# Rows of h at one place for the retention and at another for everything after it

## The chip, the cores and the metric

The kernel runs on one core of one Trainium2 chip. A core has a matrix engine (TensorE, PE in the profile; its loads of the stationary operand are shown as PEld), a vector engine (VectorE, DVE), a scalar engine (ScalarE, ACT), a general one (GpSimd, POOL) and a sync engine (SyncE, SP) that here issues the transfers. They run side by side and wait for each other by semaphores. The metric is device time in microseconds of one execution.

## The reference, cut to what matters

A trunk of two decoder layers over 256 tokens of width 2048, in float32. Layer 0 mixes tokens by retention, layer 1 by a short gated convolution; each mixer is followed by a SwiGLU feed-forward part.

```python
for i in range(DEPTH):                     # DEPTH = 2
    mod = (c_act @ w_mod[i] + b_mod[i])[:, None, :]
    sh1, sc1, g1, sh2, sc2, g2 = jnp.split(mod, 6, axis=-1)
    h = (rms_norm(x, norm1_g[i]) * (1.0 + sc1) + sh1)
    y = retention_mixer(...) if i == 0 else short_conv_mixer(...)
    x = x + g1 * y
    h = (rms_norm(x, norm2_g[i]) * (1.0 + sc2) + sh2)
    x = x + g2 * swiglu(h, ffn_w_in[i], ffn_w_out[i])
return rms_norm(x, final_g)
```

Retention has 8 heads with keys of 256 and values of 512; one projection gives q, k, v and a gate, with 12,288 columns in all. `h` is the input of each projection: 16 rows of 128 features by 256 tokens.

## The kernel before

**Precision.** Every float32 operand is split in two parts of a reduced float32 type: `hi`, the rounded value, and `lo`, what is left. A product takes hi by hi, hi by lo and lo by hi. For weights ACT makes `hi` (L313) and DVE makes `lo` (L316), in pieces of 128 x 1024, from `raw` tiles of 1 MB that SP fetches in the order of use. An activation row is one tile of 128 x 2 x 256: its hi half, then its lo half.

**Three forms of the product.** In `product` (L358, L361) the weights are loaded into the array and a whole row, 512 columns, streams past `hi`, then its hi half, 256 columns, past `lo`. It serves the output projections and the later stages. In `packed` (L398 to L400) the weights are loaded too, and the three partial products are three matmuls of 256 columns. In `by_token` (L373 to L375, called by `packed` for groups 512 columns wide: the retention's values and gates) it is the other way round: 128 tokens of h are loaded, and 512 columns of weights stream past them. Each of these lines has 512 matmuls with h in the retention.

**Stages.** The retention's input comes first, in spans of columns while h is still being made (to about 190 us), then head by head. Half of its output product stands in the middle and half at the end (to 786 us). Then come the feed-forward part of layer 0 (to 1521 us), the convolution (to 1880 us), the feed-forward part of layer 1, and the final norm.

**The rows of h.** One tile, `h_all`, holds 16 rows. `h[j]` is the view of 512 elements that starts at 512 j. A second view of the same tile, `raw_all`, has a stride of 514 elements: 2 (`ENDS`) for a shift column in hi and lo, and then a scaled row. It is used at the start of a normed projection, before the norm of x is known. While the output product before it ends, `scaled_only` writes row j of `raw_all` as soon as x[j] is ready (ACT L495 the hi half, DVE L496 the lo half). `normed` then copies the shift columns to all 16 rows at once (ACT L507, DVE L508) and multiplies the first group of columns with the scaled rows (L521 to L523). The norm's factor comes in between, and `modulated` writes the finished rows `h[j]` over the scaled ones, a few behind the matmuls that read those. This happens three times: for the feed-forward part of layer 0, for the convolution, and for the feed-forward part of layer 1. L521 and L523 stream the two shift columns as well, 258 columns, and L522 streams 256.

**What sets the order.** PE's instructions stand as the program writes them. DVE and ACT have an order by hand in the retention's start alone; elsewhere a scheduler places an instruction by priority and by what it depends on, that is by which regions of which tiles it reads and writes. The reductions for the modulation (L247, each over a 1 MB `raw` tile) are among those it fills in. Each engine runs its instructions in the built order and stops at one whose semaphores have not come. PE does not pass a matmul that waits.

**Places in the memory.** A tile `aside` of `LEFT` elements stands ahead of `h_all`, and a tile `beside` fills up behind it, so that the tiles which come later keep their places.

Of the kernel before, what the change touches and what calls it, by code (L numbers as in the profile page):

```python
# [10 lines left out]
F32 = mybir.dt.float32  # L11
F32R = mybir.dt.float32r
# [5 lines left out]
P = 128  # L18
D = 2048
S = 256  # L20
KT = D // P
# [27 lines left out]
STEPS = (8, 8, 20)  # L49
RAW_BUFS = 3  # L50
PART_BUFS = 4
LEFT, ENDS = 8, 2

Q0, K0, V0, G0 = 0, HEADS * DK, 2 * HEADS * DK, 2 * HEADS * DK + HEADS * DV
SH1, SC1, GT1, SH2, SC2, GT2 = range(6)
# [133 lines left out]
def trunk(ctx: ExitStack, tc: tile.TileContext, x_in, c_in, pos_in, w_mod, cols_in, tab_in, w_all, out):  # L189
# [12 lines left out]
    def tmp(tag, shape=(P, S), dtype=F32, pool=work, bufs=None):  # L202
        return pool.tile(list(shape), dtype, tag=tag, name=name(tag), bufs=bufs)
# [276 lines left out]
    hpool = ctx.enter_context(tc.tile_pool(name="hpool", bufs=1))  # L480

    hpool.tile([P, LEFT], F32, tag="aside", name="aside")
    h_all = hpool.tile([P, KT * (ENDS + 2 * S)], F32R, tag="h", name="h")
    hpool.tile([P, P - KT * ENDS], F32, tag="beside", name="beside")
    h = [h_all[:, 2 * S * j : 2 * S * (j + 1)].rearrange("p (a b) -> p a b", a=2) for j in range(KT)]
    raw_all = h_all.rearrange("p (k n) -> p k n", k=KT)

    def scaled_only(layer, norm, j):  # L490

        needed(layer, SC2 if norm else SC1, j)
        a = mod_a[layer][norm][:, j : j + 1]
        high, low = raw_all[:, j, ENDS : ENDS + S], raw_all[:, j, ENDS + S :]
        nc.scalar.activation(high, x[j], AF.Identity, scale=a)  # L495
        nc.vector.scalar_tensor_tensor(low, x[j], a, high.bitcast(F32), op0=ALU.mult, op1=ALU.subtract)  # L496
# [50 lines left out]
    def output(groups, act, which, last, after=None, base=None):  # L547

        layer, gate = which[0], mod_g[which[0]][which[1] == GT2]
        first, *groups = groups  # L550
        base, acc = first.ks[0] if base is None else base, None
        banks = product(first, act, base, last=False)
        for j, g in enumerate(groups):
            needed(*which, j)
            col = gate[:, j : j + 1]
            if last and j == KT - 1:
                (pt,) = packed(g, act, base)
                nc.vector.scalar_tensor_tensor(x[j], pt[:, 0, :], col, x[j], op0=ALU.mult, op1=ALU.add)
                acc = [acc, squares(None, x[j], "acc1")]
                if after:  # L560
                    after(j)
                return acc
            (pt,) = product(g, act, base, banks=banks[j : j + 1])
            t = tmp("sum", bufs=4)
            nc.vector.scalar_tensor_tensor(t, pt[:, 1, :], col, x[j], op0=ALU.mult, op1=ALU.add)
            nc.vector.scalar_tensor_tensor(x[j], pt[:, 0, :], col, t, op0=ALU.mult, op1=ALU.add)
            if last:
                acc = squares(acc, x[j])
            if after:
                after(j)  # L570


    with ExitStack() as inner:
# [357 lines left out]
        def ret_out(part, last):  # L931
            after = (lambda j: scaled_only(0, 1, j)) if last else None
            acc = output(RET_OUT[part], mid, (0, GT1), last, after, base=0)
            assert not asides
            for n in range(len(mid)):
                if ("mid", n) in tag_of:
                    free.append(tag_of.pop(("mid", n)))
            return acc

        for n, head in enumerate(HEAD_ORDER):  # L940
            projections(head)
            if n == HEADS // 2 - 1:
                ret_out(0, False)
        acc = ret_out(1, True)

    mpool = ctx.enter_context(tc.tile_pool(name="mpool", bufs=1))

# [30 lines left out]
    for i, g in enumerate(CONV_IN):  # L978
        pending += [sums(g)] if i else normed(acc, 1, 0, g)
        while len(pending) >= 3:  # L980
            pb, pc, pu = pending[:3]
            pending = pending[3:]
            j = done
            b, c, u = pb(tmp("bsum", pool=mpool, bufs=2)), pc(), pu()
# [73 lines left out]
```

## Time and profile before

| what | us |
|---|---|
| runs, median of 3 | 2629.78 (2628.91 to 2632.28) |
| the profiled execution | 2630.33 |
| its span, first to last instruction | 2628.6 |

The profile is of one execution. Its span is what the trace covers; the execution's own time lies 1.7 us above it. In a row of a group the figures after the bar are busy time, mean duration of one instruction in ns, and the idle time of the engine just before such instructions, with what ended it. A row of the timeline has start, duration, engine, line, operation and tiles; `x3` means that three were merged. A row of a window has the window, its length, the busy time and count of PE, of PEld, of DVE, of ACT and of POOL (only those of PE where the view was cut to that engine), and then the granted TensorE clock as a share of full speed, the busy share of the DMA engines, and GB/s. A matmul's duration is longer than its share of the stream, because neighbours overlap; what one costs is the pitch from its start to the start of the next.

### The profile page before, as it was taken

Reading aid. Unit: us, or ns where it says so; the run is one execution under the profiler, and the core shown is the slowest. Engines: PE = TensorE matmul, PEld = TensorE weight load, DVE = VectorE, ACT = ScalarE, POOL = GpSimd, SP = SyncE. Lnnn points to the kernel's source line nnn. Section 1 sums busy time; section 2 is a strip of 40 time slices with the busy share of each in tenths; the row PEclk is TensorE's granted clock in tenths of the full one; section 3 lists DMA queues with packets and bytes.
Section 4 is the critical chain, followed back from the end, with each engine's and each line's share of the span. In section 5 each row is a group of like instructions: output and inputs, shape, how many; then the busy total and the mean of one; then the engine's idle time right before and its main releaser. Section 6 shows DMA issues by size and latency. Waiting matters only on the chain.

```text
span 2628.6 us, 38238 instructions
## 1 busy us (share of the span) xinstructions
PE 2596.0 (99%) x15220; PEld 2301.1 (88%) x15220; DVE 1988.8 (76%) x2527; ACT 1249.2 (48%) x1788; POOL 149.8 (6%) x230
## 2 busy tenths in 40 slices
PE   7999999999999999999999999999999999999998
PEld 5888889888899888888888898888998888888887
DVE  7898878777698877777777889888887665555554
ACT  5544443444456444344444454444554443444443
POOL 0000001110000001101100001100000000000000
PEclk9999999999999999999999999999999999999999
DMA  9976668767686877777777758777777665555553
GB/s 398 386 279 239 249 246 305 284 258 274 240 297 247 322 287 275 285 284 282 284 271 278 282 214 330 288 272 268 260 268 267 252 223 192 193 191 187 187 190 127
DMA packets 96950, 687.58 MB, mean 262 GB/s; under 512 B 10753, under 2 KB 12545, under 8 KB 13825
## 3 DMA queue, kind: packets, MB, share of 16 engines
q1 hardware_dynamic: 96770, 685.13, 70.3%
q8 instruction: 119, 1.95, 0.3%
q14 instruction: 61, 0.50, 0.1%
HBM read 682.99 MB, written 2.10 MB: 261 GB/s over the span
## 4 chain that ended last, share of the span: by engine, by line
PE 76%; issue 20%; DVE 2%; DMA 1%; ACT 1%; POOL 0%; DVEq 0%; ACTq 0%; POOLq 0%
PE bank L358 34%; PE bank L361 18%; PE bank L373 4%; PE bank L374 4%; PE bank L375 4%; PE bank L400 2%; PE bank L398 2%; PE bank L399 2%; PE bank L521 1%; PE bank L523 1%; PE bank L522 1%; DVE raw L649 1%; DMA raw<-w_all 1%; DVE lo L316 1%; PE bank L876 1%
## 5 line engine op out<-in xcount | busy, mean ns | idle before, releaser
L316 DVE TENSOR_TENSOR lo<-raw,hi 128x1024 fp32r<-128x1024 f32 x912 | 1111.8, 1222 | 537.5 <-ACT hi L313 533.3
L313 ACT CAST hi<-raw 128x1024 fp32r<-128x1024 f32 x912 | 953.5, 1050 | 1066.7 <-PE bank L358 641.5
L358 PE MATMUL bank<-h,hi 128*128 128x512 f32 x3296 | 1142.8, 390 | 0.0
L361 PE MATMUL bank<-h,lo 128*128 128x256 f32 x3296 | 929.5, 282 | 0.0
L358 PEld LDWEIGHTS bank<-h,hi 128*128 128x128 f32 x3296 | 618.4, 188 | 129.5
L361 PEld LDWEIGHTS bank<-h,lo 128*128 128x128 f32 x3296 | 622.9, 189 | 0.0
L358 PE MATMUL bank<-mid,hi 128*128 128x512 f32 x1604 | 556.3, 390 | 0.0
L361 PE MATMUL bank<-mid,lo 128*128 128x256 f32 x1604 | 452.4, 282 | 0.9 <-DVE lo L316 0.9
L247 DVE SCALAR_TENSOR_TENSOR raw<-raw,cb 128x2048 f32<-128x2048 f32 x160 | 365.4, 2284 | 15.9 <-DMA raw<-w_mod 15.7
L358 PEld LDWEIGHTS bank<-mid,hi 128*128 128x128 f32 x1604 | 300.9, 188 | 63.1
L361 PEld LDWEIGHTS bank<-mid,lo 128*128 128x128 f32 x1604 | 303.1, 189 | 1.2 <-DVE lo L316 1.2
L373 PE MATMUL bank<-hi,h 128*128 128x512 f32 x512 | 204.4, 399 | 0.0
L374 PE MATMUL bank<-lo,h 128*128 128x512 f32 x512 | 203.8, 398 | 0.0
L375 PE MATMUL bank<-hi,h 128*128 128x512 f32 x512 | 203.6, 398 | 0.0
L358 PE MATMUL bank<-rm,hi 128*128 128x512 f32 x496 | 172.5, 390 | 0.0
L400 PE MATMUL bank<-h,lo 128*128 128x256 f32 x512 | 144.6, 282 | 8.3 <-DVE lo L316 8.3
L398 PE MATMUL bank<-h,hi 128*128 128x256 f32 x512 | 145.0, 283 | 2.5 <-ACT h L677 2.5
L399 PE MATMUL bank<-h,hi 128*128 128x256 f32 x512 | 144.4, 282 | 0.5 <-DVE h L678 0.5
L361 PE MATMUL bank<-rm,lo 128*128 128x256 f32 x496 | 139.8, 282 | 0.0
L375 PEld LDWEIGHTS bank<-hi,h 128*128 128x128 f32 x512 | 97.0, 189 | 23.5
L373 PEld LDWEIGHTS bank<-hi,h 128*128 128x128 f32 x512 | 97.0, 189 | 20.2
L374 PEld LDWEIGHTS bank<-lo,h 128*128 128x128 f32 x512 | 97.0, 189 | 20.1
(154 smaller groups left out, 2243.7 us busy)
## 6 DMA issues: line engine op xcount, KB each, us to landing
raw<-w_all SPq DMA_DIRECT2D x456, 1024.0 KB, 4.9
raw<-w_mod SPq DMA_DIRECT2D x192, 1024.0 KB, 5.0
x<-x_in SPq DMA_DIRECT2D x4, 512.0 KB, 5.8
out<-out SPq DMA_DIRECT2D x5, 256.0 KB, 3.4
decay<-tab_in SPq DMA_DIRECT2D x8, 128.0 KB, 2.8
out<-out SPq DMA_DIRECT2D x3, 128.0 KB, 2.5
out<-out SPq DMA_DIRECT2D x1, 384.0 KB, 2.7
cols<-cols_in SPq DMA_DIRECT2D x1, 160.0 KB, 9.0
```

The costliest lines, as they stand in the source:

```text
L247: nc.vector.scalar_tensor_tensor(raw, raw, 1.0, cb, op0=ALU.mult, op1=ALU.mult, accum_out=total)
L313: nc.scalar.copy(hi, raw)
L316: nc.vector.tensor_tensor(lo, raw, hi.bitcast(F32), op=ALU.subtract)
L358: nc.tensor.matmul(pt, hi, h, start=fresh and k == g.ks[0], stop=False, skip_group_check=True)
L361: nc.tensor.matmul(pt[:, 1, :], lo, h[:, 0, :], start=False, stop=last and k == g.ks[-1], skip_group_check=True)
L373: nc.tensor.matmul(o, ht[:, 0, :], hi, start=first, stop=False)
L374: nc.tensor.matmul(o, ht[:, 0, :], lo, start=False, stop=False)
L375: nc.tensor.matmul(o, ht[:, 1, :], hi, start=False, stop=last)
L398: nc.tensor.matmul(pt, hi, h[:, 0, :], start=first, stop=False, skip_group_check=True)
L399: nc.tensor.matmul(pt, hi, h[:, 1, :], start=False, stop=False, skip_group_check=True)
L400: nc.tensor.matmul(pt, lo, h[:, 0, :], start=False, stop=last, skip_group_check=True)
L521: nc.tensor.matmul(pt, hi, high, start=k == 0, stop=False, skip_group_check=True)
```

## The change

`h_all` grows by 16 elements (`LATER`), and its place is chosen so that element 16 lies where element 0 lay, seen in a grid of 512 bytes. `raw_all` starts at element 16. The rows `h[j]` start at element 0, 64 bytes lower, while the retention's projections run, and at element 16 from the end of the retention's output product on. Tiles allocated later move up by 512 bytes. No instruction is added or taken away.

```diff
-LEFT, ENDS = 8, 2
+LEFT, ENDS, LATER = 120, 2, 16
...
     hpool.tile([P, LEFT], F32, tag="aside", name="aside")
-    h_all = hpool.tile([P, KT * (ENDS + 2 * S)], F32R, tag="h", name="h")
-    hpool.tile([P, P - KT * ENDS], F32, tag="beside", name="beside")
-    h = [h_all[:, 2 * S * j : 2 * S * (j + 1)].rearrange("p (a b) -> p a b", a=2) for j in range(KT)]
-    raw_all = h_all.rearrange("p (k n) -> p k n", k=KT)
+    h_all = hpool.tile([P, LATER + KT * (ENDS + 2 * S)], F32R, tag="h", name="h")
+    hpool.tile([P, 2 * P - LEFT - LATER - KT * ENDS + 8], F32, tag="beside", name="beside")
+
+    def rows_at(o):
+        return [
+            h_all[:, o + 2 * S * j : o + 2 * S * (j + 1)].rearrange("p (a b) -> p a b", a=2) for j in range(KT)
+        ]
+
+    h = rows_at(0)
+    raw_all = h_all[:, LATER:].rearrange("p (k n) -> p k n", k=KT)
...
         acc = ret_out(1, True)
+        h = rows_at(LATER)
```

`h` is read at the time of each call, so `normed`, `modulated` and `sums` use the new list from there on.

## The prediction, on record before the changed kernel ran

> **What bounds the kernel now.** I read the page first, then the rate of TensorE (PE) in single stages, then the three places at which the built order of instructions differs.
>
> ```profile
> span 2628.6 us, 38238 instructions
> ...
> PE 2596.0 (99%) x15220; PEld 2301.1 (88%) x15220; DVE 1988.8 (76%) x2527; ACT 1249.2 (48%) x1788; POOL 149.8 (6%) x230
> ...
> L358 PE MATMUL bank<-h,hi 128*128 128x512 f32 x3296 | 1142.8, 390 | 0.0
> L361 PE MATMUL bank<-h,lo 128*128 128x256 f32 x3296 | 929.5, 282 | 0.0
> ...
> L358 PE MATMUL bank<-mid,hi 128*128 128x512 f32 x1604 | 556.3, 390 | 0.0
> ...
> L373 PE MATMUL bank<-hi,h 128*128 128x512 f32 x512 | 204.4, 399 | 0.0
> ...
> L358 PE MATMUL bank<-rm,hi 128*128 128x512 f32 x496 | 172.5, 390 | 0.0
> ...
> L398 PE MATMUL bank<-h,hi 128*128 128x256 f32 x512 | 145.0, 283 | 2.5 <-ACT h L677 2.5
> ```
>
> PE is busy through 99% of the span, with hardly any idle time before its lines. So the end is set by two things alone: the pitch from one matmul's start to the next, and each stop of PE. The last column of the L373 row is zero idle. The change touches both: the pitch, because rows of h that PE reads lie elsewhere, and the stops, because instructions change places.
>
> The pitch is read from starts in the timeline, since the mean duration holds latency. In order: packed rows (L398 to L400), value and gate columns by token (L373 to L375), and the product of the later stages (L358, L361).
>
> ```profile
> 455.72 0.28 PE L398 MATMUL bank<-h,hi 128*128 128x256 f32 x1
> ...
> 456.42 0.28 PE L398 MATMUL bank<-h,hi 128*128 128x256 f32 x1
> ...
> 457.46 0.40 PE L373 MATMUL bank<-hi,h 128*128 128x512 f32 x1
> ...
> 458.86 0.40 PE L373 MATMUL bank<-hi,h 128*128 128x512 f32 x1
> ```
> ```profile
> 859.91 0.39 PE L358 MATMUL bank<-h,hi 128*128 128x512 f32 x1
> 860.14 0.28 PE L361 MATMUL bank<-h,lo 128*128 128x256 f32 x1
> ...
> 861.30 0.39 PE L358 MATMUL bank<-h,hi 128*128 128x512 f32 x1
> ```
>
> Six packed matmuls take 0.70 us, 116.7 ns each; six by token take 1.40 us, 233.3 ns each. In the product the 512-wide one takes 0.23 us and four pairs take 1.39 us, so the same width costs about 5 ns less than by token.
>
> **The change, part by part: the place of h.** In the built program the split weights hi and lo start 352 bytes past a multiple of 512. The rows of h start at 384, and in the retention at 320 afterwards. The rows that later stages read keep 384, as do mid and the retention's own tiles, which move up by just 512 bytes. That move is free as far as the trace can tell: rows of h, and the tiles of mid and rm, sit on different multiples of 512, and all their L358 have one length, 390 ns in the three rows above. So only the retention's 3 x 512 packed and 3 x 512 by-token matmuls can change pitch, 1536 of each.
>
> No row of before has h at 320, so both terms are bounded.
>
> - By token, h is the loaded operand and the weights stream. Lower end: the attention's product L876, also 512 wide.
>
> ```profile
> 224.80 1.30 PE L876 MATMUL bank<-v,sp 128*128 128x512 f32 x5
> ```
>
> Five of these span 1.30 us; less one duration of 0.39 us, that is 0.91 us over four pitches, 227.5 ns: -5.8 ns a matmul, -8.9 us in all. Upper end: the product's saving with its sign turned, +5 ns, +7.7 us.
> - In the packed rows h streams. Lower end: half of the L876 pitch for half the columns, 113.8 ns, -2.9 ns, -4.5 us. For rows at other places there is the normed product (L521 to L523), whose 16 rows each lie 8 bytes further in the 64-byte grid:
>
> ```profile
> 786.40:820.00 33.60, 33.60 (x284) 1.00 0.63 223
> ```
>
> 33.60 us over 284 is 118.3 ns, +1.6 ns, +2.5 us; the upper end I take is again +5 ns, +7.7 us.
>
> I take zero for both. The shift is a whole 64 bytes, so an alignment finer than that is what it was. If instead the distance between stream and loaded operand decides (stream minus loaded, in bytes: product +32, by token -32 now), the change swaps the two: by token gets the product's +32 and gains 7.7 us, packed gets -32 and loses as much. Both readings end near zero.
>
> **The reordering.** All PE instructions keep their order. What moves is the pair of small copies (L507 on ACT, L508 on DVE) that put the shift column and its remainder ahead of every row of the normed product. With the rows now a slice inside a larger tile, they stand behind the scaled rows in the built order and wait for them. The first L521 waits for the DVE copy, and PE runs in order, so everything on PE stands behind it. Three places, each with the same test: when does the work now ahead of the copy end, and when does PE come to L521? A DVE instruction starts 0.08 us before the listed end of the one ahead (785.67 + 0.48 = 786.15, next start 786.07), and the copy lasts 0.18 us.
>
> After the retention:
>
> ```profile
> 779.98 0.18 DVE L508 TENSOR_TENSOR h<-s,h 128x16 fp32r<-128x16 f32 x1
> ...
> 785.67 0.48 DVE L496 SCALAR_TENSOR_TENSOR h<-x,a,h 128x256 fp32r<-128x256 f32 x1
> 786.07 2.28 DVE L247 SCALAR_TENSOR_TENSOR raw<-raw,cb 128x2048 f32<-128x2048 f32 x1
> ...
> 788.28 0.48 DVE L558 SCALAR_TENSOR_TENSOR x<-bank,g,x 128x256 f32<-128x256 f32 x1
> ```
> ```profile
> 786.34 0.28 PE L521 MATMUL bank<-h,hi 128*128 128x258 f32 x1
> ```
>
> Now the copy ends at 780.16, 6 us ahead. Afterwards it stands behind row 14's remainder (L496), the modulation's reduction (L247, 2.28 us) and the last update of x (L558): 788.28 + 0.48 - 0.08 + 0.18 = 788.86. PE is there at 786.34: a stop of 2.5 us.
>
> After the first feed-forward part:
>
> ```profile
> 1518.18 0.48 DVE L496 SCALAR_TENSOR_TENSOR h<-x,a,h 128x256 fp32r<-128x256 f32 x1
> 1519.48 1.23 DVE L316 TENSOR_TENSOR lo<-raw,hi 128x1024 fp32r<-128x1024 f32 x1 [0.82 <-ACT hi L313]
> ```
> ```profile
> 1521.08 0.28 PE L521 MATMUL bank<-h,hi 128*128 128x258 f32 x1
> ```
>
> The copy moves past some 110 DVE instructions but lands behind this L316: 1519.48 + 1.23 - 0.08 + 0.18 = 1520.81, before 1521.08. No stop, with 0.27 us to spare: that cover gone, it costs what it is late.
>
> After the convolution:
>
> ```profile
> 1877.89 0.18 DVE L508 TENSOR_TENSOR h<-s,h 128x16 fp32r<-128x16 f32 x1
> ...
> 1880.06 0.48 DVE L558 SCALAR_TENSOR_TENSOR x<-bank,g,x 128x256 f32<-128x256 f32 x1
> ...
> 1882.14 0.48 DVE L496 SCALAR_TENSOR_TENSOR h<-x,a,h 128x256 fp32r<-128x256 f32 x1
> ```
> ```profile
> 1879.78 0.28 PE L521 MATMUL bank<-h,hi 128*128 128x258 f32 x1
> ```
>
> Here it lands behind row 15's remainder: 1882.14 + 0.48 - 0.08 + 0.18 = 1882.72, 2.9 us after 1879.78. Row 15 itself needs the last update of x, which waits for PE's last matmul of the group before, so this stop cannot shrink by DVE being early.
>
> On ACT the copy of 0.22 us waits for the same rows; behind it stand casts that PE's progress releases later, so it adds nothing. The queues of SP and POOL keep their order. Sum of stops: 5.4 us, at PE's full price, since PE has no later idle to give it back.
>
> **The clock after a stop.** Gaps of this length are there in the retention's start:
>
> ```profile
> 39.70:42.10 2.40, 0.32 (x3) 0.12 (x1) 2.40 (x4) 0.91 (x1) 0.00 (x0) 1.00 1.03 430
> 42.10:47.70 5.60, 5.54 (x35) 5.00 (x36) 4.99 (x6) 3.04 (x7) 0.00 (x0) 1.00 1.01 421
> 47.70:50.00 2.30, 0.32 (x3) 0.12 (x1) 2.30 (x3) 1.06 (x3) 0.00 (x0) 1.00 1.01 413
> 51.00:55.00 4.00, 4.00 (x18) 3.41 (x17) 2.36 (x2) 4.00 (x9) 0.00 (x0) 0.57 1.00 414
> 153.30:155.50 2.20, 0.29 (x4) 0.09 (x2) 2.20 (x5) 1.75 (x4) 0.00 (x0) 1.00 0.00 0
> 156.00:160.00 4.00, 4.00 (x18) 3.44 (x18) 4.00 (x5) 1.55 (x3) 0.00 (x0) 0.60 0.83 307
> 1817.60:1818.70 1.10, 0.35 (x3) 0.03 (x1) 1.10 (x3) 0.99 (x4) 0.00 (x0) 1.00 0.00 0
> 1818.70:1823.00 4.30, 4.18 (x24) 3.73 (x25) 4.30 (x8) 1.13 (x3) 0.00 (x0) 1.00 0.25 63
> ```
>
> In each row the granted clock is the third number from the end. Of three gaps of some 2 us, two were followed by 4 us at 0.57 and 0.60 (153.30: 4 x 0.40 = 1.6 us lost); the gap at 1817.60, half as long, was not. The new stops are longer, so I take three chances in four at 1.6 us for each of two: 2.4 us, between 0 and 3.2.
>
> The Trainium skill (TensorE: Matmul & The Clock Gate, Part 1: The HAM clock gate) says that the clock falls back to half only after an idle window of about 3.4 us. By that rule stops of 2.5 and 2.9 us would cost no clock, and the sum would be 5.4 us; the rows above, with 2 us gaps that did cost it, decide.
>
> **Sum.** 5.4 + 2.4 + 0 = 7.8 us on the profiled execution's 2630.33 us (span 2628.6): 2638.1. The median of the runs is 0.55 us lower, so 2637.6 us.
>
> **The rivals.**
> - *By token takes the product's pitch, packed keeps its own*: -7.7 us, 2629.9. For it: its distance becomes the product's +32. Against it: the streamed operand, the weights, does not move.
> - *Faster: the new place ends a slowdown of both streams.* Both reach the L876 pitch, -8.9 - 4.5 = -13.4 us, 2624.2. It decides from 13.1 us on, where the stops are paid and 0.2% is left over. For it: no pitch of before is proven the least. Against it: L876 reaches it in a few matmuls only, and both terms have to come at once. The Trainium skill (the same page, Back-to-back issue gap) gives N / 2.4 + 2.5 ns between warm matmuls, 216 ns at 512 columns; by it the by-token part alone could save an estimated 27 us. No row of before comes near that.
> - *Packed alone pays*: its stream gets the distance -32 and +5 ns, +7.7 us, 2645.3. For it: by token, at -32, is slower than the product. Against it: the normed product's rows lie all over the grid and lose 1.6 ns.
> - *The change does not do what it says*: pitch as it was, and the copies early after all, 2629.8. Against it: the built order and the semaphore that L521 waits for.
>
> **How the numbers follow.** Forecast 0.45 (own range 2635 without any clock loss, to 2641); by token alone 0.22; both faster, or more than that, 0.17; packed pays 0.13; nothing 0.03. What a measurement of this kernel can tell from no change is 0.2%, 5.3 us: 2624.5 to 2635.0. So slower 0.45 + 0.13 = 0.58, same 0.22 + 0.03 = 0.25, faster 0.17. The range runs from 2624, which leaves out the better half of the faster case, to 2647, beyond the case in which packed pays.
>
> **What would show it.** Idle time of PE before the first normed matmul: about 2.5 us near 786 and 2.9 us near 1880, released by the DVE copy, and none near 1521; a granted clock near 0.6 within some 5 us after each; pitches of 233 and 117 ns in the retention, and 0.347 us for the product's pair. The forecast is wrong if either retention pitch moves by more than 2 ns, or if L521 starts on time.

## The result, and the profile after

| kernel | median, us | runs |
|---|---|---|
| before, on the same chip | 2631.03 (2628.91 to 2632.36) | 13 |
| after | 2638.04 (2632.70 to 2642.77) | 13 |

The ratio is 1.0028, with a 95% interval of 1.0019 to 1.0036: the change costs 7.4 us, between 5.0 and 9.5. The forecast was slower, 2637.6 us. The profiled execution after took 2636.04 us, with a span of 2634.3, 5.7 us above that of before.

The page of after, in its part on busy time and its groups (busy time, mean ns, idle time before with its releaser):

```profile
span 2634.3 us, 38235 instructions
...
PE 2596.6 (99%) x15220; PEld 2301.6 (87%) x15220; DVE 1990.6 (76%) x2527; ACT 1249.3 (47%) x1788; POOL 145.9 (6%) x230
...
L373 PE MATMUL bank<-hi,h 128*128 128x512 f32 x512 | 203.5, 397 | 0.0
...
L398 PE MATMUL bank<-h,hi 128*128 128x256 f32 x512 | 145.2, 284 | 2.5 <-ACT h L685 2.5
```

PE's busy time has grown by 0.6 us while the span has grown by 5.7, and the durations of the matmuls have hardly moved (L373 397 ns where it was 399, L398 284 where it was 283). So most of the time went into waiting, and the waits of PE name it (waiter, what it waited for: us in total, times, longest). Lines behind the change's insertion are 8 higher: the first normed product is now L529, the DVE copy of the shift column L516.

```profile
PE bank L400 <- DVE lo L316: 9.2, 6, 2.2
PE bank L529 <- DVE h L516: 5.0, 2, 2.9
```

The second row is new: two waits for the copy, 5.0 us together. Here are both, and the place between them that was to stay free. First PE, with what ended its idle time in brackets:

```profile
785.47 0.28 PE L400 MATMUL bank<-rm,lo 128*128 128x256 f32 x1
787.82 0.36 PE L529 MATMUL bank<-h,hi 128*128 128x258 f32 x1 [2.06 <-DVE h L516]
...
1524.58 0.28 PE L400 MATMUL bank<-mid,lo 128*128 128x256 f32 x1
1524.70 0.28 PE L529 MATMUL bank<-h,hi 128*128 128x258 f32 x1
...
1882.48 0.28 PE L400 MATMUL bank<-mid,lo 128*128 128x256 f32 x1
1885.68 0.36 PE L529 MATMUL bank<-h,hi 128*128 128x258 f32 x1 [2.92 <-DVE h L516]
```

Without a stop the first L529 starts 0.12 us after the last L400, as at 1524.58. So the stops, measured from start to start, are 785.47 + 0.12 to 787.82, 2.23 us, and 1882.48 + 0.12 to 1885.68, 3.08 us: 5.3 in all. The bracket counts from the modelled end of the matmul before, which is why it is smaller.

Then DVE in the same stretches:

```profile
784.49 0.48 DVE L504 SCALAR_TENSOR_TENSOR h<-x,a,h 128x256 fp32r<-128x256 f32 x1
784.88 2.28 DVE L247 SCALAR_TENSOR_TENSOR raw<-raw,cb 128x2048 f32<-128x2048 f32 x1
...
787.09 0.48 DVE L566 SCALAR_TENSOR_TENSOR x<-bank,g,x 128x256 f32<-128x256 f32 x1
787.49 0.18 DVE L516 TENSOR_TENSOR h<-s,h 128x16 fp32r<-128x16 f32 x1
...
1524.25 0.18 DVE L516 TENSOR_TENSOR h<-s,h 128x16 fp32r<-128x16 f32 x1
...
1882.88 0.48 DVE L566 SCALAR_TENSOR_TENSOR x<-bank,g,x 128x256 f32<-128x256 f32 x1
...
1884.95 0.48 DVE L504 SCALAR_TENSOR_TENSOR h<-x,a,h 128x256 fp32r<-128x256 f32 x1
1885.35 0.18 DVE L516 TENSOR_TENSOR h<-s,h 128x16 fp32r<-128x16 f32 x1
```

The copy stands just where the built order put it: behind the last update of x at 787, behind a piece of weights at 1524 (done 0.27 us before PE comes), behind row 15's remainder at 1885.

The granted clock around each stop (window, its length, PE's busy time and count, clock, DMA share, GB/s), with three windows of the retention's start:

```profile
27.00:31.00 4.00, 3.99 (x28) 1.00 1.01 420
...
51.55:54.96 3.41, 3.41 (x12) 0.50 1.01 418
...
156.00:160.00 4.00, 4.00 (x29) 1.00 0.80 291
...
785.42:788.83 3.41, 1.34 (x11) 1.00 0.84 322
788.83:792.24 3.41, 3.41 (x18) 0.50 0.92 348
...
1881.09:1884.51 3.42, 1.67 (x15) 1.00 1.01 376
1884.51:1887.92 3.41, 2.24 (x19) 1.00 0.88 322
1887.92:1891.33 3.41, 3.41 (x32) 1.00 0.37 154
```

After the first stop the clock fell to half for 3.41 us, 3.41 x 0.50 = 1.7 us lost; after the longer one it did not.

The windows at the stops are cut where the clock changes or could change, for the traces show a grid. In each of the fourteen traces the stretches at half clock (the one after the last matmul left aside) last 3.41 us each and start whole steps of 3.4133 us apart: in after at 51.55 and 788.83, 737.28 us or 216 steps; in before at 27.10, 51.00 and 156.81, 7 and 31 steps. So the clock is set in pieces of 3.41 us, on a grid that lies differently in each execution, and a piece runs at half clock when PE idled through enough of the piece before. The first stop lies whole in one piece, of which PE works 1.34 us, and the next runs at half clock. The longer stop is split at 1884.51: PE works 1.67 and 2.24 us of the two pieces, and the clock stays full.

And two stretches at a low clock that before had in the retention's start are not there in this execution: 156 to 160, at 0.60 in the prediction's row, and 27 to 31, which stood so in before:

```profile
27.00:31.00 4.00, 3.99 (x16) 0.57 1.01 420
```

Last the pitch in the retention, from starts 452 to 462 us into after:

```profile
453.16 0.28 PE L398 MATMUL bank<-h,hi 128*128 128x256 f32 x1
...
455.29 0.28 PE L398 MATMUL bank<-h,hi 128*128 128x256 f32 x1
...
456.34 0.39 PE L373 MATMUL bank<-hi,h 128*128 128x512 f32 x1
...
461.94 0.39 PE L373 MATMUL bank<-hi,h 128*128 128x512 f32 x1
```

18 packed matmuls in 2.13 us are 118.3 ns each, where before had 116.7; 24 by token in 5.60 us are 233.3 ns, as before. Over all undisturbed ones of the retention (those within 20 ns of these values) the means went from 116.91 to 118.27 ns and from 233.26 to 232.92 (by token gained some 1.5 ns in the first 192 us alone). With 1536 of each that is +2.1 - 0.5 = +1.6 us.

### The profile page after: what moved, and what is told of

It reads as the page before. It is cut to its first block, busy times and chain, and to the rows that moved or that the text cites. A ratio compares the mean times of both kernels' runs of the same rounds, so it can differ in the third digit from the quotient of the medians.

```text
span 2634.3 us, 38235 instructions
## 1 busy us (share of the span) xinstructions
PE 2596.6 (99%) x15220; PEld 2301.6 (87%) x15220; DVE 1990.6 (76%) x2527; ACT 1249.3 (47%) x1788; POOL 145.9 (6%) x230
## 5 line engine op out<-in xcount | busy, mean ns | idle before, releaser
L316 DVE TENSOR_TENSOR lo<-raw,hi 128x1024 fp32r<-128x1024 f32 x912 | 1112.5, 1223 | 544.4 <-ACT hi L313 539.8
L373 PE MATMUL bank<-hi,h 128*128 128x512 f32 x512 | 203.5, 397 | 0.0
L374 PE MATMUL bank<-lo,h 128*128 128x512 f32 x512 | 202.6, 396 | 0.0
L400 PE MATMUL bank<-h,lo 128*128 128x256 f32 x512 | 144.7, 283 | 9.2 <-DVE lo L316 9.2
L398 PE MATMUL bank<-h,hi 128*128 128x256 f32 x512 | 145.2, 284 | 2.5 <-ACT h L685 2.5
L374 PEld LDWEIGHTS bank<-lo,h 128*128 128x128 f32 x512 | 96.3, 188 | 20.2
L373 PEld LDWEIGHTS bank<-hi,h 128*128 128x128 f32 x512 | 96.4, 188 | 20.0
```

Source lines behind the costliest of these rows:

```text
L316: nc.vector.tensor_tensor(lo, raw, hi.bitcast(F32), op=ALU.subtract)
L373: nc.tensor.matmul(o, ht[:, 0, :], hi, start=first, stop=False)
L374: nc.tensor.matmul(o, ht[:, 0, :], lo, start=False, stop=False)
L398: nc.tensor.matmul(pt, hi, h[:, 0, :], start=first, stop=False, skip_group_check=True)
L400: nc.tensor.matmul(pt, lo, h[:, 0, :], start=False, stop=last, skip_group_check=True)
```

## The experiments

Four of them pull the two halves of the change apart. The copies get a place of their own in the program, ahead of scaled row 14, so that they cannot fall behind it (the same diff in all that are marked "early copies"):

```diff
-LEFT, ENDS, LATER = 120, 2, 16
+LEFT, ENDS, LATER, ENDS_AT = 120, 2, 16, 14
...
+    def shift_ends(layer, norm):
+
+        needed(layer, SH2 if norm else SH1)
+        shift = mod_s[layer][norm].unsqueeze(2)
+        ends = [raw_all[:, :, i : i + 1] for i in range(ENDS)]
+        nc.scalar.copy(ends[0], shift)
+        nc.vector.tensor_tensor(ends[1], shift, ends[0].bitcast(F32), op=ALU.subtract)
+
     def scaled_only(layer, norm, j):
 
+        if j == ENDS_AT:
+            shift_ends(layer, norm)
...
-        needed(layer, SH2 if norm else SH1)
-        shift = mod_s[layer][norm].unsqueeze(2)
-        ends = [raw_all[:, :, i : i + 1] for i in range(ENDS)]
-        nc.scalar.copy(ends[0], shift)
-        nc.vector.tensor_tensor(ends[1], shift, ends[0].bitcast(F32), op=ALU.subtract)
```

The last five lines come out of `normed`. In the runs of this section before had medians of 2630.02, 2628.90, 2629.86 and 2630.93 us.

**place_only**: early copies, h at 320 in the retention as in after.

> The rows of h keep their lower place during the retention, but the two copies of the shift column are written in the program ahead of row 14's scaled row, so that they stand early in the built order again. Theory (the time comes from the two stops and the half clock after them, the place is worth nothing in sum): no stop at the first normed matmul, pitches of 118 ns packed and 231 to 233 ns by token as after the change, and a time within 2 us of before, about 2631. Rival (the place of h costs it): still some 7 us over before, about 2638.

2630.26 us, ratio 1.0004 (0.9995 to 1.0012). Its timeline of PE at the end of the retention and of the convolution has no stop (L534 is the first normed product here):

```profile
787.48 0.28 PE L400 MATMUL bank<-rm,lo 128*128 128x256 f32 x1
787.59 0.28 PE L534 MATMUL bank<-h,hi 128*128 128x258 f32 x1
...
1880.69 0.28 PE L400 MATMUL bank<-mid,lo 128*128 128x256 f32 x1
1880.81 0.28 PE L534 MATMUL bank<-h,hi 128*128 128x258 f32 x1
```

Packed runs at 118.28 ns, by token at 232.89, as in after. So the place is worth between -1.3 and +3.2 us; the rivals of -7.7, +7.7 and -13.4 us all fall.

**order_only**: after's order with h at the old place (384) from the start.

```diff
-    h = rows_at(0)
+    h = rows_at(LATER)
```

> The tile keeps its new size, place and views, but h is read at the old place, 384, from the start; the built order is that of the changed kernel. Theory: both stops, 2.2 and 3.1 us from pitch to pitch, pitches of 116.7 and 233.3 ns in the retention, and a time some 7 us over before, about 2638. Rival (the place of h costs it): the time of before, 2631, with stops that are given back later.

2638.45 us, ratio 1.0028 (1.0013 to 1.0043, 6 runs): the whole loss. Pitches are those of before, 116.94 and 233.25 ns. Its waits of PE:

```profile
PE bank L529 <- DVE h L516: 5.3, 2, 2.9
```

The profiled execution is the fastest of the six, 2631.39 us. It had both stops, and no low clock in the windows right behind them:

```profile
786.00:790.00 4.00, 4.00 (x37) 1.00 0.97 317
...
1881.00:1885.00 4.00, 3.96 (x33) 1.00 0.80 334
```

**neither**: early copies and h at 384 from the start, so both halves undone.

> Both undone: h at the old place and the copies written ahead of row 14; the control for what writing the copies earlier does by itself. Theory: no stop, pitches of 116.7 and 233.3 ns, time of before within 1.5 us, about 2631; against the run with the lower place alone it shows the place by itself, forecast within 2 us of it. Rival: more than 3 us off before, so that the early writing has a price of its own.

2628.31 us, ratio 0.9996 (0.9987 to 1.0005): no change, as it should be, so the new place of the copies in the program costs nothing of itself. Beside this run, which has the same early copies, the median of place_only is 2.0 us higher and its mean 1.3 us: that is the place by itself, within the forecast 2 us, and hardly clear of the scatter.

**at_256**: early copies, h another 64 bytes lower.

```diff
-LEFT, ENDS, LATER, ENDS_AT = 120, 2, 16, 14
+LEFT, ENDS, LATER, ENDS_AT = 104, 2, 32, 14
```

> Early copies, and the rows of h in the retention another 64 bytes lower, 256 past a multiple of 512. Theory (a shift by whole 64 bytes is worth little): pitches within 2 ns of 117 packed and 233 by token, time within 3 us of before. Rival (the distance between the stream and the loaded operand decides): a pitch that differs by 5 ns or more in one of the two forms, 7.7 us.

2631.64 us, ratio 1.0007 (0.9998 to 1.0016); by token 233.4 ns, packed 118.1. Nothing that can be told from no change.

**first_stop** and **third_stop**: h at 384, early copies, but at one of the three places they stay in `normed`, as in after.

```diff
-        if j == ENDS_AT:
+        if j == ENDS_AT and (layer, norm) != (0, 1):
             shift_ends(layer, norm)
...
+        if (layer, norm) == (0, 1):
+            shift_ends(layer, norm)
```

(third_stop has (1, 1) in both lines.)

> h at the old place throughout; the copies are early for the second and the third normed product and late for the first. Theory: a stop of 2.2 to 2.7 us near 786, none near 1880, and in part of the executions a stretch of half clock behind it worth 1.7 us; of the 7 us over before (or 8 to 10 over the run with neither) this one gives 2.5 to 4.5. Rival (a stop is given back later, or only one of the two counts): within 1 us of the run with neither.

> The mirror: late copies for the third normed product alone. Theory: a stop of 3.1 us near 1880 and none near 786; 3 to 5 us over the run with neither, and the two prices add up to that of both. Rival: within 1 us of the run with neither.

2633.42 us, ratio 1.0014 (1.0005 to 1.0023), and 2634.66 us, 1.0015 (1.0006 to 1.0025). The two add up to 0.29%, and both together cost 0.28%. In the profile of first_stop (L536 is the first normed product, L504 the DVE copy) and then in that of third_stop:

```profile
786.68 0.28 PE L400 MATMUL bank<-rm,lo 128*128 128x256 f32 x1
789.12 0.36 PE L536 MATMUL bank<-h,hi 128*128 128x258 f32 x1 [2.15 <-DVE h L504]
```
```profile
1880.65 0.28 PE L400 MATMUL bank<-mid,lo 128*128 128x256 f32 x1
1883.84 0.52 PE L536 MATMUL bank<-h,hi 128*128 128x258 f32 x1 [2.92 <-DVE h L504]
```

The same stops as in after, 2.3 and 3.1 us by the 0.12 us of above. The clock did the opposite of what it did there: it stayed after the first and fell after the third (1.7 us lost). By the grid of 3.41 us the first is split here, at 788.21 (PE works 2.16 and 2.50 us of the two pieces), and the third lies whole in one, as the windows of third_stop show.

```profile
1880.47:1883.88 3.41, 0.49 (x5) 1.00 0.99 303
1883.88:1887.29 3.41, 3.41 (x16) 0.50 0.92 382
```

**at_352** and **at_128**: early copies, h at the place in 512 bytes where hi and lo begin (`LEFT, LATER = 128, 8`), and 224 bytes below it (72, 64).

> Early copies, h in the retention at 352, 32 bytes lower than before, so that it is no longer at a multiple of 64 and begins at the same place in the 512-byte grid as the weights. Theory (the fine alignment counts, whole steps of 64 do not): packed rows, where h streams, go the way of a misaligned stream, up to 122 ns, and by token stays within 2 ns of 233. Rival (place is worth nothing at any step): 117 and 233 within 1.5 ns.

> Early copies, h in the retention at 128, four steps of 64 lower. Theory: as at 320 and 256, 117 to 118.5 ns packed and 231 to 234 by token. Rival (distance to the weights decides): 5 ns or more off in one of the two.

One execution each: 2621.16 us and 2628.66 us, beside 2628.90 for before. At 128 both pitches are those of before (233.29 and 116.88 ns). At 352 by token fell to 227.99 ns as a mean and packed rose to 119.61. This I had not expected: by token was to stay within 2 ns of 233.

**at_352_timed**, **always_352**, **at_368**, **at_368_timed**: the same kernel timed; h at 352 after the retention too (`LATER` 0); h 16 bytes above 352 (`h = rows_at(4)` in place of `rows_at(0)`), run once and then timed.

> The kernel of at_352 again, now timed: h at byte 352 of 512 while the weights of retention move past it, at 384 from the output product on, the copies of the shift ahead of row 14. If its one time of 2621.16 us is the work of the place, the median is 2620 to 2623 us, a ratio of 0.9965 to 0.9975, because every multiplication by token after 192 us is about 6 ns shorter (1552 of them in all: 9 us off, 2 us back on the packed ones). If it was chance of one execution, the ratio is 0.999 to 1.0005, as that of the kernel called neither.

> As at_352, but h stays at byte 352 of 512 from the output product on as well (LATER is 0), so scaled rows and shift columns lie 32 bytes lower than in at_352. If only the multiplications by token gain by lying at the place of the weights, by token stays at 227 ns, packed at 119.6 in retention, and the median is within 1 us of at_352_timed. If the products between (258 and 512 columns, which read the scaled rows) gain as well, it is 2 to 6 us below at_352_timed; if they lose as the packed ones do, 2 to 4 us above it.

> As at_352, with h 16 bytes higher (368 of 512) during retention. If what counts is that h and the weights begin at the same place of 64 bytes, the 16 bytes undo it: by token goes back to about 233 ns and the time to 2628 to 2630 us. If the pitch falls with the distance, by token is about 230 ns and the time about 2625 us. If it is only that h is not at 32 bytes from them, by token stays at 227 ns and the time at 2621 to 2623 us.

> The kernel of at_368 again, now timed. Some 1550 multiplications by token at 229.5 ns in place of 233.3 and some 1660 packed ones at 117.5 in place of 116.9 make 5.8 us less and 0.9 us more than before: a ratio of about 0.998 (0.9975 to 0.9987), about 1 us below at_352 by the same sum. If 16 bytes from the weights' place gave no more than the one look's chance, the ratio is 0.999 to 1.0005.

| kernel | median, us | ratio | by token, ns | packed, ns |
|---|---|---|---|---|
| at_352_timed | 2624.93 | 0.9978 (0.9968 to 0.9988) | 228.02 | 119.62 |
| always_352 | 2626.59 | 0.9983 (0.9974 to 0.9992) | 228.06 | 119.61 |
| at_368 (one execution) | 2622.98 | | 229.52 | 117.48 |
| at_368_timed | 2624.99 | 0.9980 (0.9971 to 0.9989) | 230.46 | 117.59 |

at_352_timed beats both kernels, but misses the forecast 2620 to 2623 us: the one execution of at_352 was at the fast end (the nine timed runs go from 2621.52 to 2626.49). By pitch the saving is 1536 x 5.2 = 8.0 us by token less 1536 x 2.7 = 4.1 us packed, 3.9 us; the ratio says 5.8, from 3.2 to 8.4. Its timeline of PE, packed and then by token:

```profile
430.30 0.28 PE L398 MATMUL bank<-h,hi 128*128 128x256 f32 x1
...
451.90 0.28 PE L398 MATMUL bank<-h,hi 128*128 128x256 f32 x1
...
452.96 0.40 PE L373 MATMUL bank<-hi,h 128*128 128x512 f32 x1
...
468.61 0.39 PE L373 MATMUL bank<-hi,h 128*128 128x512 f32 x1
```

180 packed matmuls in 21.60 us are 120.0 ns each, 69 by token in 15.65 us are 226.8 ns. always_352 is no better than at_352_timed, nor clearly worse: 1.7 us in the median lies between the forecasts. Its trace says that the products between gain nothing: the three matmuls of a normed product keep their pitch within 0.2 ns. In the later product the one of 512 columns got 2.6 ns dearer and that of 256 cheaper by as much, so ten pairs took 3.47 us in both kernels (859.89 to 863.36, and 859.67 to 863.14 in at_352_timed). at_368 is as good within the intervals, and its mean of 229 to 230 ns is not one speed but two. In the timeline of at_368_timed:

```profile
269.18 0.39 PE L373 MATMUL bank<-hi,h 128*128 128x512 f32 x1
...
274.62 0.39 PE L373 MATMUL bank<-hi,h 128*128 128x512 f32 x1
275.10 0.50 PE L374 MATMUL bank<-lo,h 128*128 128x512 f32 x1
...
276.36 0.39 PE L373 MATMUL bank<-hi,h 128*128 128x512 f32 x1
...
287.56 0.39 PE L373 MATMUL bank<-hi,h 128*128 128x512 f32 x1
```

The first 24 take 5.44 us, 226.7 ns each. Then L374 starts 0.25 us late: it waited for a piece of `lo` (DVE L316). Behind it 48 take 11.20 us, 233.3 each. In at_368, the same program, this stretch had no such wait and ran at 226.7 to its end. Other stretches of at_368_timed have one speed throughout, with the same rows of h: 69 from 453.55 us on take 16.10 us, 233.3 each, and 69 from 643.77 us on take 15.64, 226.7 each. So two speeds exist, and the place shifts the share of each. In this one case a wait turned one into the other in mid-stretch, so the addresses alone do not pick it; whether it is the moment of the restart, or the buffer or bank of a stretch, was not tried.

## Why the prediction was right

The forecast was made against the profiled execution, so the table follows it through: start of the first normed product after each stage, and the span, all in us from the span's start.

| kernel | retention done | feed-forward 0 done | convolution done | span |
|---|---|---|---|---|
| before | 786.34 | 1521.08 | 1879.78 | 2628.6 |
| after | 787.82 | 1524.70 | 1885.68 | 2634.3 |
| difference by stage | +1.48 | +2.14 | +2.28 | -0.20 |
| place_only | 787.59 | 1522.33 | 1880.81 | 2629.3 |
| order_only | 785.59 | 1520.41 | 1881.04 | 2629.6 |
| third_stop | 787.93 | 1522.67 | 1883.84 | 2633.9 |

The first difference is the stop of 2.23 us less 0.75: two stretches at a low clock are missing from the retention's start (3.4 us), against the dearer pitch (1.6 us, all in this stage) and about 1 us of stalls, which differ between executions there. The second is the low clock after the stop, 1.7 us, and 0.4 more. The third is the stop of 3.08 less 0.80.

- *The bound: PE's pitch and PE's stops.* Right. Both remain the only places where time moved.
- *The reordering is what costs.* Right, and shown: order_only has the whole loss without the move of h, place_only has the move without the loss. Why the scheduler ties the copies to the scaled rows once those are a slice inside a larger tile was read from the built order; it was not tried alone.
- *Three places, stops of 2.5, 0 and 2.9 us.* Right in place and cause; the measured stops are 2.23, 0 and 3.08 us. Both errors have names. A term was left out: from the end of the copy (787.49 + 0.18 = 787.67) to L529 at 787.82 pass 0.15 us, and the same after 1885.35 + 0.18. And at the first place row 14's remainder came earlier than in the execution of before: 784.49 is 1.10 us ahead of the moment PE would have come (785.59), 785.67 was 0.67 ahead of 786.34. So 0.43 us less, 0.15 more. The sum, 5.3 us, agrees with 5.4.
- *No stop near 1521, with 0.27 us to spare.* Right to the hundredth: 1524.70 less 1524.43. But the release of 0.15 us, left out here too, takes more than half of it: 0.12 us were to spare.
- *The clock, 2.4 us.* Right in mechanism and in the price of a stretch, 1.7 us. The chance of three in four is not refuted. The prediction counted three gaps in the start of before and two stretches at half clock; a fourth gap, 1.87 us long and ended at 27.01, was followed by the row at 27 to 31, so it was three of four. Of the six stops of 2.2 us and more in the profiles of after, order_only, first_stop and third_stop only two were followed by half clock, and the grid of 3.41 us tells which: those that lay whole in one piece (PE works 1.34 us of it in after, 0.49 in third_stop). The other four were split, and PE worked 1.67 us or more of each piece (at the least 1.67 in after, 2.16 in first_stop, 1.75 and 1.92 in order_only). The fourteen traces agree, from 24 us on, where their record of the clock begins: the 23 pieces in which PE idled 1.84 us or more were all followed by half clock, none with 1.71 us or less was, and of the six between two were. If a stop meets the grid at random, the two stops, with 2.06 and 2.92 us of idle time in after and a threshold of 1.8 us, have chances of about 0.55 and 0.8, which is 2.3 us in all (an estimate from these figures). Over all runs the mean granted clock is 0.9963 after and 0.9969 before (its runs beside the experiments), which is 0.0006 x 2634 = 1.6 us, and the scatter of the runs leaves 0.2 to 3.0 open. The Trainium skill (TensorE: Matmul & The Clock Gate, Part 1: The HAM clock gate) would have had no loss, since the stops are below its idle window of about 3.4 us; the row at 788.83 stands against it.
- *The place of h, 0.* The step that was off: "the shift is a whole 64 bytes, so an alignment finer than that is what it was". Packed does not return to its pitch after a shift of 64 bytes, it pays 1.3 ns (118.27 and 118.28 in the two kernels at 320, 116.88 to 117.03 at 384 and 128). Nor did the reading by the distance between the operands hold, by which the pitches would have moved by 5 ns each way. The net of +1.6 us by pitch is within both terms' bounds, and place_only's +1.1 us (ratio 1.0004) does not differ from it.
- *PE has no later idle to give it back.* Almost. The 0.80 us of the third stage come from a wait of before at 1817.56, which is smaller after: the timelines of PE in before and then in after have

```profile
1817.56 0.39 PE L358 MATMUL bank<-mid,hi 128*128 128x512 f32 x1
1818.82 0.39 PE L361 MATMUL bank<-mid,lo 128*128 128x256 f32 x1 [0.87 <-DVE lo L316]
```
```profile
1821.18 0.39 PE L358 MATMUL bank<-mid,hi 128*128 128x512 f32 x1
1821.65 0.39 PE L361 MATMUL bank<-mid,lo 128*128 128x256 f32 x1
```

From 1.26 us between the two starts to 0.47. But neither, which has no stop, is also 0.5 us quicker in that stage than before, so it is not shown that the stop gave this back.

The sum by what was measured: 5.3 (stops) + 1.6 (clock) + 1.6 (pitch) = 8.5 us, up to 0.8 of it possibly given back, beside 7.4 (5.0 to 9.5) in the ratio. With the clock's term known only from 0.2 to 3.0 us, and 1.6 us of pitch that the forecast put at nothing, the 5.3 us of the stops are what was foreseen; that 7.8 came so near to 7.4 is in part luck.

## What to carry to other kernels

When an edit changes only a view or an address, compare the built order of instructions first: here the addresses were worth 1 us or so, and a 0.18 us copy that fell behind other work on DVE cost 7. On an engine that is busy 99% of the span, find for every instruction that it waits for the work that stands ahead of it, and add what a stop brings after itself: the release (0.15 us here) and, where PE idles for some 1.8 us within one piece of the clock's grid, 3.41 us at half clock (1.7 us here). An instruction that depends on nothing late belongs early in the program by hand, where no region of a tile can tie it to later writers.

## What was not expected of the hardware

- A by-token matmul, 512 streamed columns, has two speeds here, 226.8 and 233.3 ns, at the same granted clock and with no wait inside a stretch. With h and the weights beginning at the same place of 64 bytes (352) it was nearly always the faster one after 192 us; with 32 bytes between them (384, 320, 256, 128) it was the slower one; at 16 bytes it changed from stretch to stretch, and once within a stretch, behind a wait of 0.25 us. The packed form, 256 columns, moves the other way: 116.9 to 117.0 ns at 384 and 128, 118.1 to 118.3 at 256 and 320, 119.6 at 352.
- Whether the clock falls after a stop of PE does not follow from the stop's length alone: it fell after 2.23 us in after and 3.08 us in third_stop, and not after 2.3 us in first_stop, 2.57 and 3.08 in order_only, or 3.08 in after. What separates them in these traces is how the stop lies on a grid of 3.4133 us: the clock of a piece was half when PE had idled for 1.84 us or more of the piece before. Where the grid lies in an execution cannot be foreseen, so for a single stop it remains a chance.
